# Reading the streamed operand from its last column down, with the split weights at shifting places, in a two-block transformer kernel

## The chip, the cores and the metric

The kernel runs on one core of one Trainium2 chip. The metric is the device time of one execution in microseconds. A comparison of two kernels on this problem tells differences of about 2% from no change.

## The reference

Two transformer blocks run one after the other on 256 tokens of width 2048, all in float32. The first has a gated linear recurrence, sliding-window attention and a feed-forward network with adaptive scales; the second a gated linear attention and a feed-forward network. Nearly all arithmetic is in products of 256 tokens with large weight matrices:

```python
h = modulate(rms_norm(x, norm1_g[l]), sh1, sc1)      # mod = silu(c) @ ada_w + ada_b
proj = h @ w_in[l] + b_in[l]
...
merged = gate_lru * (y_lru @ w_lru_out[l]) + gate_attn * (y_attn @ w_attn_out[l])
x = x + g1 * (merged @ w_o[l])
h2 = modulate(rms_norm(x, norm2_g[l]), sh2, sc2)
gate, up = jnp.split(h2 @ w_ffn_in[l], 2, axis=-1)
x = x + g2 * ((jax.nn.silu(gate) * up) @ w_ffn_out[l])
...
proj = h @ w_in                                       # second block, gla_w_in
...
return o.astype(h.dtype) @ w_out                      # gla_w_out
...
return (jax.nn.silu(g) * u) @ w_down                  # ffn_w_gu, ffn_w_down
```

## The kernel before

**Chunks.** Every large weight matrix is streamed once, in chunks of 512 input rows by 512 output columns (1 MB). `load` brings a chunk into `raw` (three buffers, on the SP queue). `split` turns it, in two halves of 128 x 1024, into two numbers of reduced precision that TensorE takes in one pass: ScalarE writes `hi`, a rounded copy (L165), and VectorE writes `lo = raw - hi` (L167). `hi` and `lo` have three buffers each. The activations lie in SBUF in the same form, `src.hi` and `src.lo`, four tiles of 256 tokens to a chunk.

**Matmuls.** `accumulate` adds a chunk's product to two PSUM banks, with three products in place of one: hi x hi, hi x lo, lo x hi. There are two forms:

- By token (`tokens=True`): the activations of 128 tokens are the stationary operand and 512 columns of weights stream past them. Lines 182, 183 and 184, 24 matmuls of 512 columns a chunk. The gate and up projections (`fgps`, `fups`), the values (`gvps`) and group 13 of `w_in` go this way.
- By feature: 128 columns of weights are stationary and the 256 tokens stream past. Lines 189, 191 and 193, 48 matmuls of 256 columns a chunk. All other weights go this way (`part`, `aops`, `ups`, `gps`, `glps`, `lops`, `wops`, `fops`, `gkps`, `gqps`, `grps`, `ggps`).

A group is the run of chunks whose products add up in the same two banks: 4 chunks mostly, 5 or 6 for `fops`. In all there are 464 chunks.

**Around the stream.** Small work (attention, the recurrence, norms) is cut into generators that `pump` advances between chunks. Their own matmuls, such as `sps` (L360, L361), `rps` (L570, L571) and `lrps` (L785 to L787, with 16 columns of weights), stand between those of the stream. The product of `c` with `ada_w` runs on VectorE: `matvec` loads a 512 KB strip into `mvw` (L234, pool of `MVS` buffers) and adds it, scaled, into `mva` (L239). Its first 16 steps come before any matmul; later ones are spread over the chunks, on the POOL queue and then on the SP queue between the loads of `raw`. A scheduler with priorities orders the instructions; `lead` moves the loads and splits ahead.

The pools around the change:

```python
SLOTS, MVS, RAWS, HIS, LOS = 24, 6, 3, 3, 3
mvw = ctx.enter_context(tc.tile_pool(name="mvw", bufs=MVS))
hip = ctx.enter_context(tc.tile_pool(name="hip", bufs=HIS))
lop = ctx.enter_context(tc.tile_pool(name="lop", bufs=LOS))
```

Of the kernel before, what the change touches and what calls it, by code (L numbers as in the profile page):

```python
# [12 lines left out]
F32R = mybir.dt.float32r  # L13
# [5 lines left out]
P = 128  # L19
# [3 lines left out]
NG = NK // 4  # L23
EPS = 1e-6
PREP = 2000
SLOTS, MVS, RAWS, HIS, LOS = 24, 6, 3, 3, 3
NEG = -3.0e38
HEADS = 16
KVH = 4
# [20 lines left out]
def block_pair_kernel(ctx: ExitStack, tc: tile.TileContext, a: dict):  # L50
    nc = tc.nc
# [7 lines left out]
    hip = ctx.enter_context(tc.tile_pool(name="hip", bufs=HIS))  # L59
    lop = ctx.enter_context(tc.tile_pool(name="lop", bufs=LOS))  # L60
# [8 lines left out]
    def f32(ap):  # L69
        return ap.bitcast(F32)  # L70
# [21 lines left out]
    def halves(t):  # L92
        return [t[:, 0:2, :], t[:, 2:4, :]]
# [56 lines left out]
    def load(ap):  # L150
        raw = rawp.tile([P, 4, 512], F32, tag="raw", name="raw")
        nc.sync.dma_start(raw, ap)
        return raw

    lead = [0]

    def split(ap):

        parts = []
        with tc.high_priority(offset=lead[0]):  # L160
            raw = load(ap)
            for b in range(2):
                rb = raw[:, 2 * b:2 * b + 2, :]
                hi = hip.tile([P, 2, 512], F32R, tag="hi", name="hi")
                nc.scalar.activation(hi, rb, AF.Copy)  # L165
                lo = lop.tile([P, 2, 512], F32R, tag="lo", name="lo")
                nc.vector.tensor_tensor(lo, rb, f32(hi), ALU.subtract)  # L167
                parts.append((hi, lo))
        return parts

    def accumulate(ps, ap, src, first, last, tokens=False):

        parts = split(ap)
        for kk in range(4):
            hi, lo = parts[kk // 2]
            wk = kk % 2
            fst, lst = first and kk == 0, last and kk == 3
            if tokens:
                for t in range(2):
                    tsl = slice(t * P, (t + 1) * P)  # L180
                    xh, xl = src.hi(kk)[:, tsl], src.lo(kk)[:, tsl]
                    nc.tensor.matmul(ps[t], xh, hi[:, wk, :], start=fst, stop=False)  # L182
                    nc.tensor.matmul(ps[t], xh, lo[:, wk, :], start=False, stop=False)  # L183
                    nc.tensor.matmul(ps[t], xl, hi[:, wk, :], start=False, stop=lst)  # L184
                continue
            for f in range(4):
                wsl = slice(f * P, (f + 1) * P)
                o = ps[f // 2][:, f % 2, :]
                nc.tensor.matmul(o, hi[:, wk, wsl], src.hi(kk), start=fst and f % 2 == 0,  # L189
                                 stop=False, skip_group_check=True)  # L190
                nc.tensor.matmul(o, hi[:, wk, wsl], src.lo(kk), start=False, stop=False,  # L191
                                 skip_group_check=True)
                nc.tensor.matmul(o, lo[:, wk, wsl], src.hi(kk), start=False, stop=lst,  # L193
                                 skip_group_check=True)

    def banks(name, tokens=False):
        return [bank(name, [P, 512] if tokens else [P, 2, T]) for _ in range(2)]

    def project(chunks, src, name, tokens=False):


        ps = banks(name, tokens)
        n = len(chunks)
        for c in range(n):
            accumulate(ps, chunks[c], src[c], c == 0, c == n - 1, tokens)
            if c < n - 1:
                pump()
        return ps

    def chunks_of(wname, g, ks=None):  # L210
        w = a[wname]
        return [w[g, k] for k in (range(w.shape[1]) if ks is None else ks)]
# [44 lines left out]
    def ada_steps(strip, queue=nc.gpsimd):  # L257


        def done(ps):  # L260
            if strip < 4:
                cols = ((16 + 4 * strip, 0, 4), (4 * strip, 4, 4))
            else:
                cols = ((8 * strip, 0, 8),)
            for j, p, n in cols:
                nc.vector.tensor_tensor(mod[:, j:j + n], ps[:, p:p + n], v("ada_b", j, n), ALU.add)

        return matvec([a["ada_w"][strip, k] for k in range(NK)], lambda k: cact[:, k:k + 1],
                      1024, done, queue)
# [149 lines left out]
    first = ada_steps(0, nc.sync)  # L419
# [36 lines left out]
    for q in range(NG):  # L456
# [3 lines left out]
        for g, ks in plan[q]:  # L460
            tok = g == 13
            if g in held:
                if q == 0:
                    early[g] = banks(f"e{g}", tok)
                ps = early[g]
            else:
                ps = banks("part")
            for k in ks:
                if g in held:
                    accumulate(ps, a["w_in"][g, k], h[k], k == 0, k == NG - 1, tok)  # L470
                else:
                    accumulate(ps, a["w_in"][g, k], h[k], k == ks[0], k == ks[-1])
                for st in ahead[:share]:
                    st()
                if ahead and len(ahead) <= share:
                    next_h()
                ahead = ahead[share:]
                lead[0] = PREP
                if q == NG - 1 and k < ks[-1]:
                    pump()  # L480
            if g not in held:
# [8 lines left out]
                ps = halves(early[g])  # L490
# [20 lines left out]
    for f in range(NG):  # L511
        ps = banks("aops")
# [96 lines left out]
    for f in range(NG):  # L609
# [4 lines left out]
        ps = project(chunks_of("w_lru_out", f), y_lru, "lops")  # L614
# [20 lines left out]
    for f in range(NG):  # L635
        ps = project(chunks_of("w_o", f), merged, "wops")
# [219 lines left out]
    for g in range(2):  # L856
        kg = slot("gk")
        ps = project(chunks_of("gla_w_in", 2 + g), h, "gkps")
# [6 lines left out]
        ps = project(chunks_of("gla_w_in", g), h, "gqps")  # L865
# [9 lines left out]
    for hd in range(GH):  # L875
        vg = slot("gv", shape=[P, 2, 512])
        ps = project(chunks_of("gla_w_in", 4 + hd), h, "gvps", True)
# [36 lines left out]
    for hd in range(GH):  # L914
        ps = project(chunks_of("gla_w_in", 8 + hd), h, "grps")
# [12 lines left out]
    for f in range(NG):  # L928
        ps = banks("ggps")
# [136 lines left out]
```

## Time and profile before

| | |
|---|---|
| time, median of 2 runs | 2779.15 us (2778.5 to 2779.8) |
| the profiled execution | 2775.35 us, span 2773.6 us |
| mean granted TensorE clock | 0.999 |
| busy: TensorE, weight loads, VectorE, ScalarE | 98%, 90%, 64%, 48% |
| moved by DMA | 602 MB, 217 GB/s in the mean |

The span runs from the first to the last instruction. A row of the timeline gives start and duration in microseconds, engine, line, operation, the tiles written and read, and shape and count. PE rows are matmuls, PEld rows the loads of the stationary operand. Matmuls are pipelined, so their durations overlap; how fast they go is read from start to start. A row of waits names who waited for whom, the sum in microseconds, the number of times and the longest.

### The profile page before, as it was taken

How to read it: one execution, taken by the hardware profiler on the slowest of the kernel's cores; microseconds unless marked ns; L12 is line 12 of the kernel's file. 1: busy time of each engine (PE TensorE's matmuls, PEld its weight loads, DVE VectorE, ACT ScalarE, POOL GpSimd, SP SyncE). 2: the span in 40 equal slices, each digit the busy share in tenths (PEclk: the TensorE clock that was granted, in tenths of full speed). 3: DMA queues.
4: the chain of work that ended last, by engine and by line, in shares of the span. 5: the costliest groups of instructions: out<-in, count | busy, mean ns of one | idle time of the engine just before them, and what ended most of it. 6: DMA issues, size and time to landing. Idle time of an engine off the chain costs nothing.

```text
span 2773.6 us, 43912 instructions
## 1 busy us (share of the span) xinstructions
PE 2710.8 (98%) x18612; PEld 2489.2 (90%) x18612; DVE 1784.8 (64%) x2000; ACT 1321.3 (48%) x1531; POOL 25.7 (1%) x52
## 2 busy tenths in 40 slices
PE   4999999999999999999999999999999999999999
PEld 4999899999999788899888999899988889988899
DVE  8887966977876865444444677866654444444544
ACT  3446537873445444434444555555554443344443
POOL 1100000000000000000000000000000000000000
PEclk9999999999999999999999999999999999999999
DMA  9974784768875776555555544445555555555554
GB/s 364 368 301 149 261 324 175 282 241 324 326 283 181 271 259 217 180 190 193 183 192 186 190 169 168 147 144 182 192 188 182 183 190 189 198 182 189 185 196 160
DMA packets 100165, 602.00 MB, mean 217 GB/s; under 512 B 11120, under 2 KB 11632, under 8 KB 40576
## 3 DMA queue, kind: packets, MB, share of 16 engines
q1 hardware_dynamic: 93056, 574.03, 58.2%
q0 software_dynamic: 6912, 25.17, 2.3%
q8 instruction: 145, 2.38, 0.3%
q14 instruction: 52, 0.43, 0.0%
HBM read 597.06 MB, written 2.10 MB: 216 GB/s over the span
## 4 chain that ended last, share of the span: by engine, by line
PE 91%; DVE 5%; ACT 1%; issue 1%; DMA 1%; SPq 0%; DVEq 0%; ACTq 0%
PE fops L189 6%; PE fops L191 6%; PE fops L193 6%; PE fgps L184 6%; PE fgps L183 6%; PE fgps L182 6%; PE fups L184 5%; PE fups L183 5%; PE fups L182 5%; DVE lo L167 2%; PE part L189 2%; PE part L191 2%; PE part L193 2%; DVE mva L239 1%; DMA mvw<-ada_w 1%
## 5 line engine op out<-in xcount | busy, mean ns | idle before, releaser
L167 DVE TENSOR_TENSOR lo<-raw,hi 128x1024 fp32r<-128x1024 f32 x928 | 1134.4, 1223 | 899.3 <-ACT hi L165 897.5
L165 ACT ACTIVATE hi<-raw 128x1024 fp32r<-128x1024 f32 x928 | 982.8, 1060 | 1285.8 <-PE fups L184 280.6
L189 PE MATMUL fops<-hid,hi 128*128 128x256 f32 x1408 | 389.0, 276 | 0.0
L193 PE MATMUL fops<-hid,lo 128*128 128x256 f32 x1408 | 388.8, 276 | 0.0
L191 PE MATMUL fops<-hid,hi 128*128 128x256 f32 x1408 | 388.8, 276 | 0.0
L183 PE MATMUL fups<-lo,h 128*128 128x512 f32 x704 | 275.9, 392 | 0.9 <-DVE lo L167 0.9
L184 PE MATMUL fups<-hi,h 128*128 128x512 f32 x704 | 276.7, 393 | 0.0
L182 PE MATMUL fups<-hi,h 128*128 128x512 f32 x704 | 274.2, 390 | 0.0
L184 PE MATMUL fgps<-hi,h 128*128 128x512 f32 x672 | 264.9, 394 | 0.0
L182 PE MATMUL fgps<-hi,h 128*128 128x512 f32 x672 | 264.6, 394 | 0.0
L191 PEld LDWEIGHTS fops<-hid,hi 128*128 128x128 f32 x1408 | 264.3, 188 | 0.0
L189 PEld LDWEIGHTS fops<-hid,hi 128*128 128x128 f32 x1408 | 264.3, 188 | 0.0
L193 PEld LDWEIGHTS fops<-hid,lo 128*128 128x128 f32 x1408 | 264.3, 188 | 0.0
L183 PE MATMUL fgps<-lo,h 128*128 128x512 f32 x672 | 263.3, 392 | 0.0
L239 DVE SCALAR_TENSOR_TENSOR mva<-mvw,cact,mva 128x1024 f32<-128x1024 f32 x180 | 230.2, 1279 | 18.7 <-DMA mvw<-ada_w 17.0
L183 PEld LDWEIGHTS fups<-lo,h 128*128 128x128 f32 x704 | 132.2, 188 | 31.3 <-DVE lo L167 1.3
L182 PEld LDWEIGHTS fups<-hi,h 128*128 128x128 f32 x704 | 132.2, 188 | 29.3
L184 PEld LDWEIGHTS fups<-hi,h 128*128 128x128 f32 x704 | 132.3, 188 | 27.4
L183 PEld LDWEIGHTS fgps<-lo,h 128*128 128x128 f32 x672 | 126.3, 188 | 27.4
L182 PEld LDWEIGHTS fgps<-hi,h 128*128 128x128 f32 x672 | 126.3, 188 | 26.3
L184 PEld LDWEIGHTS fgps<-hi,h 128*128 128x128 f32 x672 | 126.3, 188 | 26.0
L189 PE MATMUL part<-h,hi 128*128 128x256 f32 x512 | 145.6, 284 | 0.1
(322 smaller groups left out, 5440.6 us busy)
## 6 DMA issues: line engine op xcount, KB each, us to landing
raw<-w_in SPq DMA_DIRECT2D x88, 1024.0 KB, 4.9
raw<-w_ffn_in SPq DMA_DIRECT2D x88, 1024.0 KB, 4.8
raw<-ffn_w_gu SPq DMA_DIRECT2D x88, 1024.0 KB, 4.8
mvw<-ada_w SPq DMA_DIRECT2D x144, 512.0 KB, 6.5
raw<-gla_w_in SPq DMA_DIRECT2D x48, 1024.0 KB, 4.8
raw<-w_ffn_out SPq DMA_DIRECT2D x44, 1024.0 KB, 4.9
raw<-ffn_w_down SPq DMA_DIRECT2D x44, 1024.0 KB, 4.9
mvw<-ada_w POOLq DMA_DIRECT2D x48, 512.0 KB, 8.4
```

The costliest lines, as they stand in the source:

```text
L165: nc.scalar.activation(hi, rb, AF.Copy)
L167: nc.vector.tensor_tensor(lo, rb, f32(hi), ALU.subtract)
L182: nc.tensor.matmul(ps[t], xh, hi[:, wk, :], start=fst, stop=False)
L183: nc.tensor.matmul(ps[t], xh, lo[:, wk, :], start=False, stop=False)
L184: nc.tensor.matmul(ps[t], xl, hi[:, wk, :], start=False, stop=lst)
L189: nc.tensor.matmul(o, hi[:, wk, wsl], src.hi(kk), start=fst and f % 2 == 0, stop=False, skip_group_check=True)
L191: nc.tensor.matmul(o, hi[:, wk, wsl], src.lo(kk), start=False, stop=False, skip_group_check=True)
L193: nc.tensor.matmul(o, lo[:, wk, wsl], src.hi(kk), start=False, stop=lst, skip_group_check=True)
L239: nc.vector.scalar_tensor_tensor(state["acc"], w, col(k), state["acc"], ALU.mult, ALU.add)
```

## The change

The matmuls of `accumulate` take the moving operand with a step of -1, from the last column to the first, and address the PSUM bank in the same manner, so that each result lands where it did. The stationary operand is taken as before. The buffers of `hi` and `lo` get 128 elements more, and `halfbuf` puts the half at one of four starts in its buffer, 0, 16, 32 or 48 elements; `next_place` chooses a pair of starts for each group, sixteen pairs in turn, counted apart for the two forms. The room for it comes from `mvw`, which has five buffers in place of six.

```diff
-SLOTS, MVS, RAWS, HIS, LOS = 24, 6, 3, 3, 3
+SLOTS, MVS, RAWS, HIS, LOS = 24, 5, 3, 3, 3
...
+    place = {}
+    groups = [0, 0]
+
+    def next_place(tokens):
+        n = groups[tokens]
+        groups[tokens] += 1
+        place["hi"], place["lo"] = 16 * (n % 4), 16 * ((n // 4 + n) % 4)
+
+    def halfbuf(pool, name):
+        t = pool.tile([P, 1024 + P], F32R, tag=name, name=name)
+        return t[:, place[name]:place[name] + 1024].rearrange("p (b n) -> p b n", b=2)
+
     def split(ap):
...
-                hi = hip.tile([P, 2, 512], F32R, tag="hi", name="hi")
+                hi = halfbuf(hip, "hi")
                 nc.scalar.activation(hi, rb, AF.Copy)
-                lo = lop.tile([P, 2, 512], F32R, tag="lo", name="lo")
+                lo = halfbuf(lop, "lo")
                 nc.vector.tensor_tensor(lo, rb, f32(hi), ALU.subtract)
...
     def accumulate(ps, ap, src, first, last, tokens=False):
 
+        if first:
+            next_place(tokens)
         parts = split(ap)
...
-                    nc.tensor.matmul(ps[t], xh, hi[:, wk, :], start=fst, stop=False)
-                    nc.tensor.matmul(ps[t], xh, lo[:, wk, :], start=False, stop=False)
-                    nc.tensor.matmul(ps[t], xl, hi[:, wk, :], start=False, stop=lst)
+                    o, wh, wl = ps[t][:, ::-1], hi[:, wk, ::-1], lo[:, wk, ::-1]
+                    nc.tensor.matmul(o, xh, wh, start=fst, stop=False)
+                    nc.tensor.matmul(o, xh, wl, start=False, stop=False)
+                    nc.tensor.matmul(o, xl, wh, start=False, stop=lst)
                 continue
+            xh, xl = src.hi(kk)[:, ::-1], src.lo(kk)[:, ::-1]
             for f in range(4):
                 wsl = slice(f * P, (f + 1) * P)
-                o = ps[f // 2][:, f % 2, :]
-                nc.tensor.matmul(o, hi[:, wk, wsl], src.hi(kk), start=fst and f % 2 == 0,
+                o = ps[f // 2][:, f % 2, ::-1]
+                nc.tensor.matmul(o, hi[:, wk, wsl], xh, start=fst and f % 2 == 0,
                                  stop=False, skip_group_check=True)
-                nc.tensor.matmul(o, hi[:, wk, wsl], src.lo(kk), start=False, stop=False,
+                nc.tensor.matmul(o, hi[:, wk, wsl], xl, start=False, stop=False,
                                  skip_group_check=True)
-                nc.tensor.matmul(o, lo[:, wk, wsl], src.hi(kk), start=False, stop=lst,
+                nc.tensor.matmul(o, lo[:, wk, wsl], xh, start=False, stop=lst,
                                  skip_group_check=True)
```

The added lines move everything below them by 17 lines: L189, L191 and L193 become L206, L208 and L210, and L234 becomes L251.

The scheduler's order changes at a few places. The first is the SP queue at the start, with the waits that each load has. The DVE wait is for VectorE to free the buffer. Before:

```order
L97 DMA vec<-vec 128x436
L234 DMA mvw<-ada_w 128x1024 x6
L234 DMA mvw<-ada_w 128x1024 [waits DMAHW1_49,DVE_49]
L234 DMA mvw<-ada_w 128x1024 [waits DMAHW2_49,DMAHW0_49,DVE_49]
L234 DMA mvw<-ada_w 128x1024 [waits DMAHW3_49,DVE_49]
L234 DMA mvw<-ada_w 128x1024 [waits DMAHW4_49,DVE_49]
L423 DMA x_84<-xT 128x1024
```

After the change:

```order
L97 DMA vec<-vec 128x436
L251 DMA mvw<-ada_w 128x1024 x5
L251 DMA mvw<-ada_w 128x1024 [waits DMAHW1_49,DVE_49]
L251 DMA mvw<-ada_w 128x1024 [waits DMAHW2_49,DVE_49]
L251 DMA mvw<-ada_w 128x1024 [waits DMAHW3_49,DMAHW0_49,DVE_49]
L251 DMA mvw<-ada_w 128x1024 [waits DMAHW4_49,DVE_49]
L251 DMA mvw<-ada_w 128x1024 [waits DMAHW5_49,DVE_49]
L440 DMA x_84<-xT 128x1024
```

Five loads go out at once where it was six; the sixth waits for VectorE.

The second place is on TensorE, in the recurrence of the first block: `gps` is the stream, `rps` the two gate products of the recurrence (for each of four heads a pair). Before:

```order
L193 MATMUL gps<-h,lo 128x256
L189 MATMUL gps<-h,hi 128x256
L570 MATMUL rps<-uc,lw 128x256
L571 MATMUL rps<-uc,lw 128x256
L191 MATMUL gps<-h,hi 128x256
L193 MATMUL gps<-h,lo 128x256
L189 MATMUL gps<-h,hi 128x256
```

After the change:

```order
L206 MATMUL gps<-h,hi 128x256
L208 MATMUL gps<-h,hi 128x256
L587 MATMUL rps<-uc,lw 128x256
L588 MATMUL rps<-uc,lw 128x256
L587 MATMUL rps<-uc,lw 128x256
L588 MATMUL rps<-uc,lw 128x256
L210 MATMUL gps<-h,lo 128x256
```

The four pairs of this group stood at four places among the matmuls of the stream and now stand two by two. Elsewhere TensorE has the same sequence as before; on VectorE some steps of `mva` and `lo` change places with their neighbours.

## The prediction, made before the changed kernel was run

> **What bounds the kernel now.** I read the page from the top: busy times, slices, chain, then the groups.
>
> ```profile
> PE 2710.8 (98%) x18612; PEld 2489.2 (90%) x18612; DVE 1784.8 (64%) x2000; ACT 1321.3 (48%) x1531; POOL 25.7 (1%) x52
> ...
> PEclk9999999999999999999999999999999999999999
> ...
> PE 91%; DVE 5%; ACT 1%; issue 1%; DMA 1%; SPq 0%; DVEq 0%; ACTq 0%
> ...
> PE mvp L251 <- DVE mva L239: 36.7, 3, 34.4
> ...
> raw<-w_in SPq DMA_DIRECT2D x88, 1024.0 KB, 4.9
> ```
>
> TensorE is busy 98% of the 2773.6 us span, with 91% of the chain that ended last, and its granted clock is at the top in every slice. It stands idle at the start (34.4 us until the first matmul) and in small pieces later. So what counts is the rate at which TensorE takes matmuls. A busy matmul is pipelined: its duration overlaps the next, and the rate is the distance from start to start. That I read from the timeline, first and last row of an answer, in four stretches without waits:
>
> ```profile
> 1199.82 0.28 PE L189 MATMUL fops<-hid,hi 128*128 128x256 f32 x1
> ...
> 1221.92 0.28 PE L189 MATMUL fops<-hid,hi 128*128 128x256 f32 x1
> ```
>
> These are 196 feature matmuls (256 columns): 22.10 us over 195 distances, 113.3 ns each.
>
> ```profile
> 631.78 0.28 PE L193 MATMUL lops<-yr,lo 128*128 128x256 f32 x1
> ...
> 653.92 0.28 PE L191 MATMUL glps<-h,hi 128*128 128x256 f32 x1
> ```
>
> The same shape, 189 rows: 22.14 us over 188, 117.8 ns. So there are two paces, and a stretch keeps its pace for many chunks.
>
> ```profile
> 1469.81 0.39 PE L183 MATMUL fgps<-lo,h 128*128 128x512 f32 x1
> ...
> 1505.97 0.39 PE L182 MATMUL fups<-hi,h 128*128 128x512 f32 x1
> ...
> 154.43 0.40 PE L182 MATMUL e<-hi,h 128*128 128x512 f32 x1
> ...
> 159.33 0.40 PE L182 MATMUL e<-hi,h 128*128 128x512 f32 x1
> ```
>
> Token matmuls (512 columns): 36.16 us over 158 distances is 228.9 ns; in the early stretch 4.90 us over 21 is 233.3 ns. Going from 256 to 512 columns doubles the distance (113.3 to 228.9), so the price is per column, 0.443 to 0.447 ns, with no fixed part to save.
>
> The code gives the counts: 464 chunks of weights, of which 196 are taken by token (22 gate and 22 up groups of 4, 4 v groups of 4, and the 4 chunks of group 13), 24 matmuls each, 4,704; the other 268 by feature, 48 each, 12,864. At their faster paces they take 12,864 x 113.3 = 1457.9 us and 4,704 x 228.9 = 1076.7 us, together 2534.6 of the span. How much of the slower pace is mixed in shows in the mean durations, which follow the pace (276 where the distance is 113.3, 281 where it is 117.8):
>
> ```profile
> L191 PE MATMUL fops<-hid,hi 128*128 128x256 f32 x1408 | 388.8, 276 | 0.0
> L191 PE MATMUL lops<-yr,hi 128*128 128x256 f32 x256 | 71.9, 281 | 0.0
> L191 PE MATMUL wops<-m,hi 128*128 128x256 f32 x256 | 71.9, 281 | 0.0
> L191 PE MATMUL glps<-h,hi 128*128 128x256 f32 x256 | 71.9, 281 | 0.0
> L191 PE MATMUL ups<-h,hi 128*128 128x256 f32 x256 | 71.2, 278 | 0.0
> L191 PE MATMUL part<-h,hi 128*128 128x256 f32 x512 | 143.0, 279 | 0.0
> ```
>
> lops, wops and glps are slow throughout: three lines of 256 each, 2,304 matmuls x 4.4 ns = 10 us. ups, gps and part lie about halfway, some 3,000 matmuls at 1.5 to 2.5 ns, 5 us more. So the slow pace costs about 15 us today.
>
> **The change part by part.**
>
> *Direction.* All 17,568 weight matmuls read the moving operand and address the bank from the last column down. No matmul is added, and each result lands where it did. The trace has no operand that runs down, so the price is unknown and I bound it. Three rows stand near:
>
> ```profile
> 213.53 0.60 PE L361 MATMUL sps<-kT,e 128*128 128x256 f32 x2
> 213.97 0.38 PE L360 MATMUL sps<-kT,e 128*128 128x128 f32 x2
> ...
> L785 PEld LDWEIGHTS lrps<-h,warh x16: 93/94/98, 1643.1 to 1649.1; 128*16 128x16 f32 x16
> L785 PE MATMUL lrps<-h,warh x16: 276/276/362, 1643.1 to 1649.2; 128*16 128x256 f32 x16
> ```
>
> The two sps records of 256 columns, plain f32, take 0.44 us from start to start, 0.22 each: the slowest streaming of 256 columns here, and my upper end (each column fetched or written by itself). [...] Nearest of all is the unchanged pace: same bytes, same number of columns, still one run without gaps. I take 0.
>
> [...]
>
> *Places.* The halves start 0, 16, 32 or 48 elements later in their buffers, another pair for each of sixteen groups in turn. In feature matmuls they are the stationary operand, in token matmuls the moving one. If the weight load disturbed the stream, a short load should show a better pace. The lrps rows are that case: 16 columns of weights, loads of 94 ns in place of the 188 of fops, and yet 276 ns, the duration that goes with 113.3. So the load next to the stream doesn't set the pace, and I take 0 for feature groups. In token groups every place lies a whole number of 64 bytes from the old one; I take 0, and as bounds the two token paces, 4.4 ns a matmul or 21 us in all, which are counted under the next point.
>
> *Which pace a stretch gets.* Fast and slow stretches use the same tiles; the pace changes where other matmuls stand between:
>
> ```profile
> 521.23 0.28 PE L189 MATMUL gps<-h,hi 128*128 128x256 f32 x1
> ...
> 527.23 0.28 PE L189 MATMUL gps<-h,hi 128*128 128x256 f32 x1
> 528.12 0.67 PE L570 MATMUL rps<-uc,lw 128*128 128x256 f32 x2 [0.61 <-ACT hi L165]
> ...
> 540.04 0.28 PE L189 MATMUL gps<-h,hi 128*128 128x256 f32 x1
> ...
> 546.05 0.28 PE L193 MATMUL gps<-h,lo 128*128 128x256 f32 x1
> ```
>
> Before the rps pair 51 distances take 6.00 us (117.6 ns); a dozen microseconds behind it 53 take 6.01 (113.4). At this very place the order now puts the four rps pairs two by two, where before they stood at four places. I read the pace as a state into which TensorE falls at an interruption, so the change draws it anew: between the 15 us saved if all is fast, and, if all is slow, 12,864 x 117.8 - 1473 = +42 us and 4,704 x 233.3 - 1077 = +21 us. I take 0.
>
> *Splitting.* hi and lo are the same 928 instructions each on ScalarE and VectorE, with rows of the same length: 0.
>
> *Five buffers instead of six for ada_w.*
>
> ```profile
> SPq L152 <- DVE lo L167: 2328.9, 453, 17.2
> SPq L234 <- DVE mva L239: 47.2, 28, 4.7
> ...
> POOL mvw L234 <- DVE mva L239: 95.9, 45, 27.2
> ...
> L239 DVE SCALAR_TENSOR_TENSOR mva<-mvw,cact,mva 128x1024 f32<-128x1024 f32 x180 | 230.2, 1279 | 18.7 <-DMA mvw<-ada_w 17.0
> ```
>
> An mvw load now waits for the step five back on VectorE, not six, so it issues up to one step (1.28 us) later. Behind it on the SP queue stand the loads of raw, for which ScalarE and then TensorE wait. The cover is that SP waits 2328.9 us for lo to free raw buffers: it runs well ahead. At the lower end the cost is 0; at the upper, all 144 loads of the SP queue late by a step with no cover, 184 us. VectorE waits only 17 us for these loads today, which lies by the lower end: +2 us, most of it before the first matmul.
>
> **Sum.** Against the profiled execution, 2775.4 us (span 2773.6 and 1.8 around it): 0 + 0 + 0 + 0 + 2 = 2777. The two timed runs have a median of 2779.15, 3.8 above, so I forecast 2780, and 2755 to 2830 for this case. A measurement of this kernel tells about 2% (2723.6 and 2834.7) from no change.
>
> **Rivals.**
>
> *The slow pace everywhere.* Descending, or shifted by 64 bytes, the stream can't fall into the fast state. Place: every weight matmul. Price +63 us, 2842; it turns the verdict to slower once some nine tenths of the matmuls are affected. For it: two paces exist and the tiles don't explain them. Against: the fast one holds for most of the run, over all tiles.
>
> [...]
>
> [...]
>
> **How the numbers follow.** No effect beyond the draw of the pace: 0.59. Slow everywhere: 0.11. One column at a time or a milder loss: 0.16. Less friction: 0.14. Faster 0.14, same 0.59, slower 0.27. The range takes in the forecast's own, the slow pace and the frictionless case, 0.84, and leaves out one column at a time: 2670 to 2850. The 184 us of the buffers stay outside, as covered.
>
> **What would show it.** Right: distances of 113 or 118 and of 229 or 233 ns again, the same in all sixteen combinations, and groups with means of 276 to 284 and 390 to 394. Wrong: any other distance, or a distance that goes with the place. Wrong on the buffers: TensorE idle behind mvw, above 5 us in sum. A 512-column matmul at 0.44 us would mean one column at a time.

## The result, and the profile after

The changed kernel takes 2846.17 us (median of 2 runs, 2844.74 to 2847.6) against 2779.15: a ratio of 1.0237 (95% interval 1.022 to 1.0254), **slower**. That is inside the range that was given, but not where the forecast stood: 2780 us and no change. It is 4 us above the rival "the slow pace everywhere" (2842), which had a chance of 0.11, and 4 us under the top of the range, 2850.

The page of the changed kernel, the lines that answer to those of before (busy times, clock slices, engines on the chain that ended last):

```profile
PE 2785.9 (98%) x18612; PEld 2545.2 (89%) x18612; DVE 1790.3 (63%) x2000; ACT 1322.2 (46%) x1531; POOL 25.8 (1%) x52
...
PEclk9999999999999999999999999999999999999999
...
PE 92%; DVE 4%; DMA 2%; issue 1%; ACT 1%; POOL 0%; SPq 0%; DVEq 0%; POOLq 0%; ACTq 0%
...
L210 PE MATMUL fops<-hid,lo 128*128 128x256 f32 x1408 | 398.5, 283 | 0.0
L208 PE MATMUL fops<-hid,hi 128*128 128x256 f32 x1408 | 396.0, 281 | 0.0
...
L199 PE MATMUL fups<-lo,h 128*128 128x512 f32 x704 | 279.4, 397 | 0.0
```

The instruction counts are those of before, TensorE is as full as before, and the granted clock stays in the top tenth. What changed is the duration of a matmul: 281 to 283 ns where `fops` had 276, and 397 for this line of `fups`, which had 392 and for which the prediction set 390 to 394.

The pace itself, from start to start, comes from the timeline of the changed kernel: first and last row of four stretches without waits. Two feature stretches, with `hi` and `lo` both 0 elements into their buffers, and both 16; then two token stretches, `hi` at 32 with `lo` at 16, and both at 16.

```profile
1211.75 0.28 PE L206 MATMUL fops<-hid,hi 128*128 128x256 f32 x1
...
1232.95 0.28 PE L206 MATMUL fops<-hid,hi 128*128 128x256 f32 x1
1245.79 0.28 PE L208 MATMUL fops<-hid,hi 128*128 128x256 f32 x1
...
1266.91 0.28 PE L206 MATMUL fops<-hid,hi 128*128 128x256 f32 x1
1337.76 0.40 PE L199 MATMUL fups<-lo,h 128*128 128x512 f32 x1
...
1357.82 0.40 PE L198 MATMUL fups<-hi,h 128*128 128x512 f32 x1
1407.83 0.40 PE L200 MATMUL fgps<-hi,h 128*128 128x512 f32 x1
...
1427.94 0.40 PE L198 MATMUL fgps<-hi,h 128*128 128x512 f32 x1
```

They are 180 distances in 21.20 us, 176 in 21.12, 86 in 20.06 and 85 in 20.11: 117.8, 120.0, 233.3 and 236.6 ns. Over the whole run no pair of places has a mean below 117.8 for features or below 233.3 for tokens. The 113.3 and 228.9 ns of before have gone.

Adding up all distances of the trace (a distance far above the pace counts as a wait, less one pace) says where the 72.2 us between the spans come from. The other kernels of this table are those of the experiments below.

| | feature matmuls, mean ns (x12,863) | token matmuls, mean ns (x4,704) | waits, us | span, us |
|---|---|---|---|---|
| before | 114.53 | 229.04 | 43.3 | 2773.6 |
| after | 118.74 | 233.50 | 40.5 | 2845.8 |
| places alone, upward | 117.3 | 231.08 | about 40 | 2817.2 |
| direction alone | 118.22 | 233.28 | 35.0 | 2832.9 |
| upward, one pair of places a form | 113.5 | 227.02 | 45.1 | 2755.0 |

Features give +54.1 us (4.21 ns x 12,863), tokens +21.0 (4.46 ns x 4,704), waits -2.8: 72.3 of the 72.2.

The waits of the changed kernel (who waited for whom, sum in us, times, longest) show the five `mvw` buffers:

```profile
SPq L251 <- DVE mva L256: 59.7, 34, 4.7
...
POOL mvw L251 <- DVE mva L256: 65.9, 39, 4.1
...
PE mvp L268 <- DVE mva L256: 36.3, 2, 34.0
```

The SP queue waits 59.7 us for a buffer where it was 47.2, the POOL queue 65.9 where it was 95.9, and the first matmul still comes 34.0 us in. VectorE and ScalarE are as busy as before (1790.3 and 1322.2 us against 1784.8 and 1321.3).

### The profile page after: what moved, and what is told of

Same layout as the page of the kernel before. It is cut to its first block, busy times and chain, and to the rows that moved or that the text cites. A ratio compares the mean times of both kernels' runs of the same rounds, so it can differ in the third digit from the quotient of the medians.

```text
span 2845.8 us, 43930 instructions
## 1 busy us (share of the span) xinstructions
PE 2785.9 (98%) x18612; PEld 2545.2 (89%) x18612; DVE 1790.3 (63%) x2000; ACT 1322.2 (46%) x1531; POOL 25.8 (1%) x52
## 4 chain that ended last, share of the span: by engine, by line
PE 92%; DVE 4%; DMA 2%; issue 1%; ACT 1%; POOL 0%; SPq 0%; DVEq 0%; POOLq 0%; ACTq 0%
PE fops L210 6%; PE fops L206 6%; PE fops L208 6%; PE fgps L198 6%; PE fgps L200 6%; PE fgps L199 6%; PE fups L200 5%; PE fups L198 5%; PE fups L199 5%; PE part L208 2%; PE part L206 2%; DVE lo L180 2%; PE part L210 2%; DMA mvw<-ada_w 2%; PE grps L208 1%
## 5 line engine op out<-in xcount | busy, mean ns | idle before, releaser
L210 PE MATMUL fops<-hid,lo 128*128 128x256 f32 x1408 | 398.5, 283 | 0.0
L206 PE MATMUL fops<-hid,hi 128*128 128x256 f32 x1408 | 397.2, 282 | 0.0
L208 PE MATMUL fops<-hid,hi 128*128 128x256 f32 x1408 | 396.0, 281 | 0.0
L198 PE MATMUL fups<-hi,h 128*128 128x512 f32 x704 | 279.3, 397 | 0.0
L200 PE MATMUL fups<-hi,h 128*128 128x512 f32 x704 | 279.3, 397 | 0.0
L198 PE MATMUL fgps<-hi,h 128*128 128x512 f32 x672 | 269.7, 401 | 0.0
L200 PE MATMUL fgps<-hi,h 128*128 128x512 f32 x672 | 267.7, 398 | 0.0
L208 PEld LDWEIGHTS fops<-hid,hi 128*128 128x128 f32 x1408 | 265.6, 189 | 0.0
L206 PEld LDWEIGHTS fops<-hid,hi 128*128 128x128 f32 x1408 | 265.0, 188 | 0.0
L210 PEld LDWEIGHTS fops<-hid,lo 128*128 128x128 f32 x1408 | 264.5, 188 | 0.0
L206 PE MATMUL part<-h,hi 128*128 128x256 f32 x512 | 148.1, 289 | 0.0
```

Of the source, the lines that this page charges most:

```text
L198: nc.tensor.matmul(o, xh, wh, start=fst, stop=False)
L200: nc.tensor.matmul(o, xl, wh, start=False, stop=lst)
L206: nc.tensor.matmul(o, hi[:, wk, wsl], xh, start=fst and f % 2 == 0, stop=False, skip_group_check=True)
L208: nc.tensor.matmul(o, hi[:, wk, wsl], xl, start=False, stop=False, skip_group_check=True)
L210: nc.tensor.matmul(o, lo[:, wk, wsl], xh, start=False, stop=lst, skip_group_check=True)
```

## Experiments

The questions were: direction or places? If direction, the read of the moving operand or the write of the bank? And what about a place matters? The first four kernels answer the first two questions; they ran on one chip beside 13 runs of the kernel before, median 2777.3 us. Most differences here are under the 2% at which two kernels are told apart on this problem, so each ratio is read with its interval.

### Places alone, upward

The changed kernel with the three reversals taken out:

```diff
-                    o, wh, wl = ps[t][:, ::-1], hi[:, wk, ::-1], lo[:, wk, ::-1]
+                    o, wh, wl = ps[t], hi[:, wk, :], lo[:, wk, :]
...
-            xh, xl = src.hi(kk)[:, ::-1], src.lo(kk)[:, ::-1]
+            xh, xl = src.hi(kk), src.lo(kk)
...
-                o = ps[f // 2][:, f % 2, ::-1]
+                o = ps[f // 2][:, f % 2, :]
```

> The direction undone, the sixteen places and the five mvw buffers kept. Theory D (the direction alone sets the pace): back to 113.3 or 117.8 ns a feature matmul and 228.9 to 233.3 a token matmul, the same for every place; 2770 to 2785 us. Theory P (the places of the weights meet the other stream, whatever its direction): the pace differs by place as in the changed kernel, 117.8 to 120 ns and 233.3 to 235; 2830 to 2850 us. Between them, about 2810 us, if each has half of the 72 us.

2820.5 us, ratio 1.0156 (1.0141 to 1.0171): without the direction the places, with the five `mvw` buffers, cost 43 us. The pace now goes with the place. Four stretches of its timeline: features at (0, 0), features at (32, 32), tokens at (32, 32), tokens at (48, 48), the place of `hi` first.

```profile
1200.80 0.28 PE L206 MATMUL fops<-hid,hi 128*128 128x256 f32 x1
...
1221.99 0.28 PE L208 MATMUL fops<-hid,hi 128*128 128x256 f32 x1
1267.74 0.28 PE L208 MATMUL fops<-hid,hi 128*128 128x256 f32 x1
...
1288.94 0.28 PE L208 MATMUL fops<-hid,hi 128*128 128x256 f32 x1
1414.72 0.39 PE L199 MATMUL fups<-lo,h 128*128 128x512 f32 x1
...
1435.95 0.39 PE L200 MATMUL fups<-hi,h 128*128 128x512 f32 x1
1439.82 0.39 PE L199 MATMUL fgps<-lo,h 128*128 128x512 f32 x1
...
1459.79 0.39 PE L200 MATMUL fgps<-hi,h 128*128 128x512 f32 x1
```

187 distances of 113.3 ns, 180 of 117.8, 91 of 233.3 and 88 of 226.9. The last is faster than anything in the kernel before. Features at (0, 32) have 113.6 in the mean, at (16, 16) 118.7, at (48, 48) 119.9.

The place doesn't explain everything. One group of `gps`, at (0, 0) throughout, begins at one pace and goes on at the other after matmuls of `rps`, the last of them from 540.72 to 542.26:

```profile
527.21 0.28 PE L206 MATMUL gps<-h,hi 128*128 128x256 f32 x1
...
532.65 0.28 PE L206 MATMUL gps<-h,hi 128*128 128x256 f32 x1
542.57 0.28 PE L210 MATMUL gps<-h,lo 128*128 128x256 f32 x1
...
552.82 0.28 PE L210 MATMUL gps<-h,lo 128*128 128x256 f32 x1
```

These are 48 distances of 113.3 ns and 87 of 117.8.

### Direction alone

The kernel before, with moving operand and bank reversed as in the change, the halves where they were and six `mvw` buffers.

```diff
-                    nc.tensor.matmul(ps[t], xh, hi[:, wk, :], start=fst, stop=False)
+                    o, wh, wl = ps[t][:, ::-1], hi[:, wk, ::-1], lo[:, wk, ::-1]
+                    nc.tensor.matmul(o, xh, wh, start=fst, stop=False)
...
+            xh, xl = src.hi(kk)[:, ::-1], src.lo(kk)[:, ::-1]
...
-                o = ps[f // 2][:, f % 2, :]
+                o = ps[f // 2][:, f % 2, ::-1]
```

> Direction changed, places and the six mvw buffers as before. Theory D: all feature matmuls at 117.8 ns, all token matmuls at 233.3, as the changed kernel has them where both halves start at 0: 12,864 x 117.8 and 4,704 x 233.3 give 2836 to 2840 us. Theory P: the paces of before, 2775 to 2785 us.

2832.02 us, ratio 1.0196 (1.0179 to 1.0213): the direction costs 54.7 us by itself. A feature and a token stretch of its timeline:

```profile
1167.76 0.28 PE L192 MATMUL fops<-hid,hi 128*128 128x256 f32 x1
...
1188.96 0.28 PE L192 MATMUL fops<-hid,hi 128*128 128x256 f32 x1
1442.69 0.40 PE L185 MATMUL fgps<-lo,h 128*128 128x512 f32 x1
...
1483.99 0.40 PE L185 MATMUL fups<-lo,h 128*128 128x512 f32 x1
```

180 distances in 21.20 us are 117.8 ns, 177 in 41.30 are 233.3. So the slow paces come with the direction, without any shift. Here too one place has two of them: some feature groups, the last eight of `fops` among them, go at 120.0 ns, which brings the mean to 118.22. The two parts don't add: 54.7 + 43.2 would be 97.9, and the whole change costs 67.0 by the medians of the first comparison.

### The bank alone, and the read alone

In the first kernel only the bank is addressed downward, in the second only the moving operand is read downward; in each the columns of a product land in reversed order.

```diff
# the bank alone
-                o = ps[f // 2][:, f % 2, :]
+                o = ps[f // 2][:, f % 2, ::-1]
...
# the read alone
+            xh, xl = src.hi(kk)[:, ::-1], src.lo(kk)[:, ::-1]
```

The token form is edited in the same way in both.

> Only the bank is addressed from the last column down; the moving operand runs up, so that tokens, or columns, land in reversed order (the sums are other than the reference's). If the write into PSUM makes the pace: 117.8 and 233.3 ns, about 2838 us. If the read of the moving operand makes it: 113.3 and 228.9 ns, about 2779 us. If it is both together that matter, something between.

> Only the moving operand is read from the last column down; the bank runs up, so that tokens, or columns, land in reversed order. If the read makes the pace: 117.8 and 233.3 ns, about 2838 us. If the write makes it: 113.3 and 228.9 ns, about 2779 us.

The bank alone: 2777.12 us, ratio 1.0 (0.999 to 1.001). The read alone: 2831.61 us, 1.0196 (1.0175 to 1.0216). The groups of instructions, of the bank alone first:

```profile
L192 PE MATMUL fops<-hid,hi 128*128 128x256 f32 x1408 | 389.0, 276 | 0.0
...
L184 PE MATMUL fups<-hi,h 128*128 128x512 f32 x704 | 274.3, 390 | 0.0
```

The same groups of the read alone:

```profile
L192 PE MATMUL fops<-hid,hi 128*128 128x256 f32 x1408 | 397.4, 282 | 0.0
...
L184 PE MATMUL fups<-hi,h 128*128 128x512 f32 x704 | 279.1, 396 | 0.0
```

All of the direction's price lies in the read (1.0196, as with both reversed); a descending bank costs nothing (1.0).

### A shorter stationary operand

Does the stream slow down because it reads beside the load of the stationary operand? In these two kernels all chunks of a group but the first and the last load 16 columns in place of 128, once downward and once upward, and the sums of the other rows are left out.

```diff
+            w = P if fst or lst else 16
...
-                    tsl = slice(t * P, (t + 1) * P)
+                    tsl = slice(t * P, t * P + w)
...
-                wsl = slice(f * P, (f + 1) * P)
+                wsl = slice(f * P, f * P + w)
```

> As the kernel with the direction alone, but the stationary operand has 16 columns in place of 128, except in the first and the last tile of a group: most of the sums are left out, the streams are as long as before. Theory W (the weight load beside the stream takes turns with it at the memory): the short load meets it an eighth as often, and the pace falls to 113.3 ns or below for 256 columns, to 226 or below for 512. Theory S (the stream alone makes the pace, whatever loads beside it): 118 and 233 ns stay.

> As the kernel before, with the stationary operand cut to 16 columns in the same manner. Theory W: no slow stretches at 117.8 ns any more, 113.3 or below throughout, and token matmuls at 226.7 or below. Theory S: two paces, 113.3 and 117.8, and 228.9 as before.

Downward 2830.12 us and upward 2783.37, one run each, where 128 columns gave 2832.02 (on the chip of the first four kernels) and 2778.91. The groups by form, downward first, with the load of the stationary operand in the last row:

```profile
L193 PE MATMUL fops<-hid,hi 128*16 128x256 f32 x1280 | 358.4, 280 | 0.0
...
L185 PE MATMUL fups<-hi,h 128*16 128x512 f32 x616 | 244.2, 396 | 0.0
...
L193 PEld LDWEIGHTS fops<-hid,hi 128*16 128x16 f32 x1280 | 120.3, 94 | 29.7
```

Upward:

```profile
L190 PE MATMUL fops<-hid,hi 128*16 128x256 f32 x1280 | 353.3, 276 | 0.0
...
L183 PE MATMUL fups<-hi,h 128*16 128x512 f32 x616 | 243.5, 395 | 0.0
```

The load takes 94 ns where the full one takes 188. From one 16-column matmul to the next the means are 117.79 and 233.33 ns downward, where direction alone had 118.22 and 233.28: the short load doesn't bring the fast paces back. Upward they are 114.1 and 231.6 ns, where the kernel before had 114.5 and 229.0. So neither expectation came for tokens upward: the shorter load makes them slower, by 2.5 ns, in all their groups alike (the 395 above was 390). The length of the load isn't the cause of the slow downward read, but it is not without effect.

### Everything moved by 64 bytes

The kernel before with 16 elements of padding ahead of the activations and the weights, so that both start 64 bytes later:

```diff
+    pad = ctx.enter_context(tc.tile_pool(name="pad", bufs=1))
+    nc.vector.memset(pad.tile([P, 16], F32, name="pad"), 0.0)
```

> The kernel before, with 64 bytes (16 elements) put ahead of the pool of activations, so that activations and weights both lie 64 bytes further on. If the pace goes by where the two operands lie to each other: 113.3 or 117.8 and 228.9 ns, 2775 to 2785 us. If it goes by the place of the weights alone: as the places (16, 16) had it upward, 118.7 and 232.4 ns, 2845 to 2850 us.

2777.2 us, ratio 0.9992 (0.9982 to 1.0002), means of 114.5 and 229.05 ns, and the groups of before:

```profile
L191 PE MATMUL fops<-hid,hi 128*128 128x256 f32 x1408 | 389.0, 276 | 0.0
...
L184 PE MATMUL fups<-hi,h 128*128 128x512 f32 x704 | 274.3, 390 | 0.0
```

Moving one operand by 64 bytes costs (features at (16, 16) in the first experiment: 118.7 ns, against a mean of 114.53 before); moving both costs nothing (114.5 and 229.05 ns). At least for this shift, what counts is how the two operands lie to each other, not where they lie. That both did move follows from the order of the pools; the trace shows no addresses.

### One pair of places for each form, upward

From the first experiment I took the pairs with the best means: (0, 32) for features, (48, 48) for tokens, the other code as in that kernel, five `mvw` buffers included.

```diff
-        place["hi"], place["lo"] = 16 * (n % 4), 16 * ((n // 4 + n) % 4)
+        place["hi"], place["lo"] = (48, 48) if tokens else (0, 32)
```

> Upward, with one fixed pair of places for each form, the best of the sixteen: feature groups hi at 0 and lo at 32, token groups both at 48. If the paces of the sixteen places hold when a place is used alone: 12,864 x 113.6 and 4,704 x 227.0 ns, 12 and 9.6 us under the kernel before, 2755 to 2760 us. If the neighbours' places made them, 2770 to 2785 us.

2757.7 us (6 runs, 2755.54 to 2763.69), ratio 0.9928 (0.9914 to 0.9942): this is **faster than both kernels**. The gain is under 2%, but the interval leaves out 1, and the slowest of the six runs lies under the fastest of the 17 of the kernel before on this chip (2775.36). A feature and a token stretch of its timeline:

```profile
1142.79 0.28 PE L203 MATMUL fops<-hid,hi 128*128 128x256 f32 x1
...
1163.98 0.28 PE L205 MATMUL fops<-hid,hi 128*128 128x256 f32 x1
1453.67 0.40 PE L197 MATMUL fgps<-hi,h 128*128 128x512 f32 x1
...
1493.81 0.39 PE L197 MATMUL fups<-hi,h 128*128 128x512 f32 x1
```

187 distances of 113.3 ns and 177 of 226.8. Over the run the means are 113.5 and 227.02: features save 13.3 us, because almost no stretch is slow any more, and tokens 9.5, because of a pace that the kernel before never had.

### How far the places repeat, and how fine they are

Three kernels, run once each, map the place. The first puts both halves at nine places 64 bytes apart, upward; the second moves by single elements around the good places, upward; the third by single elements from 0, downward.

```diff
# 64 bytes apart, upward
+        place["hi"] = place["lo"] = 16 * (n % 9)
# single elements, upward
+        j = n % 16
+        place["hi"], place["lo"] = (48 + j, 48 + j) if tokens else (j, 32 + j)
# single elements, downward
+        place["hi"] = place["lo"] = n % 16
```

> Upward, both halves at the same place, 0, 16, 32 and so on to 128 elements, another for each group. If the pace goes by the distance of the two operands modulo 256 bytes: 64 and 128 repeat 0 (113.3 or 117.8 ns; 229.0), 80 repeats 16 (118.7; 232.4), 96 repeats 32 (117.8; 233.3), 112 repeats 48 (119.9; 227.0). If modulo 512 bytes: 64 to 112 have paces of their own, 128 repeats 0. If by the whole address: none repeats.

> Upward, the best pairs of places moved on by 0 to 15 elements, another for each group: feature groups (0 + j, 32 + j), token groups (48 + j, 48 + j). If whole blocks of 64 bytes decide: every j like 0, 113.5 and 226.9 ns, or j over 0 dearer by one block, up to 1.7 ns more. If single lines of 16 bytes decide: steps at j = 4, 8 and 12, with paces between 113 and 120, 227 and 236. [...]

> Downward, both halves at the same place, 0 to 15 elements, another for each group. If running down only moves the meeting of the two operands to other places: some j gets back to 113.3 and 227 ns, as upward. If running down has a price of its own: no j comes under 117.8 and 233.3 ns, and the others lie above, up to about 120 and 240; 2840 to 2860 us.

They took 2822.23, 2835.93 and 2859.55 us, beside one run of the kernel before for each: 2779.21 for the first two, 2783.07 for the third. Steps of 64 bytes, token means in ns:

| place | 0 | 16 | 32 | 48 | 64 | 80 | 96 | 112 | 128 |
|---|---|---|---|---|---|---|---|---|---|
| mean | 229.5 | 232.3 | 233.3 | 227.0 | 229.0 | 232.6 | 233.3 | 227.1 | 229.1 |

Two stretches of that kernel's timeline, at places 112 and 128:

```profile
1373.75 0.40 PE L198 MATMUL fups<-hi,h 128*128 128x512 f32 x1
...
1393.95 0.39 PE L200 MATMUL fups<-hi,h 128*128 128x512 f32 x1
1397.63 0.39 PE L198 MATMUL fgps<-hi,h 128*128 128x512 f32 x1
...
1416.86 0.39 PE L198 MATMUL fgps<-hi,h 128*128 128x512 f32 x1
```

89 distances of 227.0 ns and 84 of 228.9: the pace of 48 comes back at 112, that of 0 at 64 and 128. (At 0 two of the 21 chunks go at 233.3 and 233.5 ns and lift the mean; the others lie near 229.) Features do the same: 118.8 ns at 16 and 80, 119.9 at 48 and 112. In steps of 64 bytes the pattern so repeats every 64 elements, 256 bytes. Features at 0, 32, 64 and 128 have groups at 113.3 and at 117.8 ns and neither confirm nor contradict it.

Within these, single elements count. Two token stretches of the second kernel, at places 48 and 49:

```profile
1381.81 0.40 PE L199 MATMUL fups<-hi,h 128*128 128x512 f32 x1
...
1401.99 0.39 PE L201 MATMUL fups<-hi,h 128*128 128x512 f32 x1
1405.70 0.40 PE L199 MATMUL fgps<-hi,h 128*128 128x512 f32 x1
...
1425.92 0.40 PE L200 MATMUL fgps<-lo,h 128*128 128x512 f32 x1
```

89 distances of 226.7 ns, and 85 of 237.9 one element (4 bytes) further. The means of places 48 to 63 lie between 227.0 and 239.5 for tokens, of (0, 32) to (15, 47) between 113.6 and 120.0 for features. No stretch goes below 113.3 and 226.7. Neither expectation, whole blocks or lines, fits: the steps come from one element to the next, not only at 4, 8 and 12, and tokens reach 239.5, above the 236 that lines were given.

Downward, the means lie between 117.8 and 120.0 for features and 233.3 and 242.1 for tokens. Two token stretches, at places 15 and 0:

```profile
1367.77 0.41 PE L200 MATMUL fgps<-hi,h 128*128 128x512 f32 x1
...
1386.91 0.40 PE L198 MATMUL fgps<-hi,h 128*128 128x512 f32 x1
1389.80 0.40 PE L198 MATMUL fups<-hi,h 128*128 128x512 f32 x1
...
1410.80 0.40 PE L198 MATMUL fups<-hi,h 128*128 128x512 f32 x1
```

79 distances of 242.3 ns and 90 of 233.3. Places can make the downward read worse; no place tried makes it better than 117.8 and 233.3, 4.0% above 113.3 and 2.9% above 226.7. So the second expectation came. Tried with both halves alike were 19 of the 64 places in 256 bytes (0 to 15 here; 16, 32 and 48 in the changed kernel); that the downward read has a floor of its own is likely, not shown.

## Why the prediction was right and wrong

**The number: inside the range by luck.** The forecast was 2780 us and no change, with 2755 to 2830 for that case, which 2846.17 misses by 16 us. The range reaches to 2850 only because it takes in the rival "the slow pace everywhere", and the result lies 4 us inside that edge. The two terms that were put at 0 for the change itself, direction and places, both failed.

**What bounds the kernel: right.** TensorE's rate decided all; features and tokens hold 75.1 us of the slowdown, waits took 2.8 back.

**Direction, "I take 0": wrong, and the largest error.** Alone it costs 54.7 us (ratio 1.0196). The value was drawn from sameness: as many bytes and columns, one run without gaps. No row of before had a descending operand, and the upper end, 0.22 us for 256 columns (the `sps` records), lay about 105 ns above the mean of before, while the effect was 3.7 of 114.5 ns for a feature matmul and 4.2 of 229.0 for a token matmul, by the means of direction alone. The step that failed is the one from sameness to 0; what a few nanoseconds each are worth the prediction knew (+63 us for the slow pace everywhere). The runs show the price in the read of the moving operand: ratio 1.0196 (1.0175 to 1.0216) for the read alone.

**The descending bank, part of that 0: right.** No row of before had one, so the prediction had no measurement to go by. The bank alone gives 2777.12 us, a ratio of 1.0 (0.999 to 1.001). The price lay on the other side, in the read.

**Places, "0": wrong.** The step was: a short load beside the stream shows 276 ns, so the load next to the stream doesn't set the pace, so its place doesn't either. The second half doesn't follow from the first, and the first holds only in part: downward a load of 94 ns leaves the paces nearly as they were (117.79 and 233.33 ns against 118.22 and 233.28), upward it moves tokens from 229.0 to 231.6 ns. The `lrps` rows also hold more than their duration of 276 ns shows. In the timeline of before they run at 117.2 ns (18 distances from 1643.34 to 1645.45) and, after an interruption (a wait and `tokps`, 0.75 us), at 113.3 (24 from 1646.72 to 1649.44). Their stationary operand moves on by 64 bytes after every third matmul, and in the second stretch none of the four places costs anything. So with 16 columns the place made no difference in this form, while with 128 it did (113.6 ns at (0, 32), 119.9 at (48, 48), upward); how length and place act together no run shows. Upward the places cost 43 us; on top of the direction, by the spans, 12.9 us (2845.8 against 2832.9), of which about 6.7 are feature matmuls (0.52 ns x 12,863), 1.0 token matmuls and 5.5 waits. That "every place lies a whole number of 64 bytes from the old one" was no protection: the pattern is 256 bytes long (token means of 229.5, 232.3, 233.3, 227.0 and 229.0 ns at 0, 16, 32, 48 and 64 elements). How the two operands lie to each other moves a token matmul from 226.7 to 237.9 ns, and a load half as long moves it from 229.0 to 231.6.

**"A state into which TensorE falls": partly right.** One group at (0, 0) upward passes from 113.3 to 117.8 ns across the `rps` matmuls, and `lrps` from 117.2 to 113.3 across `tokps`, so the pace does change at interruptions. But it isn't a free draw. The changed kernel never reached the fast pace (no mean below 117.8 and 233.3 ns), and with features at (0, 32) the run is almost all fast (113.5). What the prediction listed as a sign of error, "a distance that goes with the place", is what the profile showed.

**The rival "the slow pace everywhere": nearly what came.** Of its two conditions the descending read held everywhere. The shift by itself did not: upward, features at (0, 32) and tokens at (48, 48) are fast (113.5 and 227.02 ns). Its price was +63 us; measured were 75.1 for the matmuls, because many features go at up to 120.0 rather than 117.8. Its argument against, that the fast pace holds over all tiles, held only for the upward read and the tiles' old places. The range's lower end, 2670 us, and the chance of 0.14 on "less friction" count on paces under 113.3 and 226.7 ns; no run shows one, those two being the fastest stretches at any place tried. The 0.16 on "one column at a time or a milder loss" counts on much slower matmuls, up to 0.44 us for 512 columns; no run shows these either, the slowest stretches being 120.0 ns for 256 columns and 242.3 for 512.

**Splitting and buffers: right as far as shown.** 0 for the splits (busy times above). No run takes the five buffers alone. Waits fell by 2.8 us in all, but a slower TensorE waits less: they are 35.0 us with direction alone and six buffers, against 43.3 before. At equal direction the kernels with five buffers wait longer, 45.1 against 43.3 us upward and 40.5 against 35.0 downward, with the places changed as well. That is of the size of the +2 us, and TensorE's wait for `mva` is as before (36.3 us against 36.7, nearly all of it ahead of the first matmul).

**Open.** Why the downward read is slower, whether one of the 45 places not tried would spare it, and how the two addresses act on each other, no run shows. Nor does any show what in an interruption makes one pair of places pass from one pace to the other, nor why a shorter load slows tokens upward. Reading the stationary operand downward as well was not tried.

## What to carry to other kernels

In a kernel that is a stream of thousands of matmuls on a full TensorE, measure the distance from start to start to a tenth of a nanosecond before calling a new addressing free: 4 ns each was 2% here, and mean durations (276 against 282) already showed it. Read the moving operand upward (downward the whole kernel took 1.0196 times as long); if it must be mirrored, mirror the write of the bank, which cost nothing (1.0). Where the two operands lie to each other is worth a sweep over 256 bytes: the right pair of places gave 0.7%, the sixteen pairs in turn cost 1.6%.

## What the runs showed of the hardware that I had not expected

- Reading the moving operand downward costs 2 to 3% of a matmul at unchanged places (means of 118.2 against 114.5 ns for 256 columns, 233.3 against 229.0 for 512), and 3 to 4% against the fastest place found (117.8 against 113.3, 233.3 against 226.7). Writing the bank downward costs nothing (1.0, 0.999 to 1.001).
- The pace of a matmul depends on how its two operands lie to each other, with a period of 256 bytes in steps of 64 (token means of 229.0 and 229.1 ns at 64 and 128 elements, 227.0 and 227.1 at 48 and 112), and with differences from one element to the next (226.7 and 237.9 ns for neighbouring places), though a common shift of 64 bytes doesn't matter (0.9992, 0.9982 to 1.0002).
- A shorter load of the stationary operand (94 in place of 188 ns) doesn't bring the fast paces back downward (117.79 and 233.33 ns) and slows token matmuls upward (231.6 against 229.0).
- At one pair of places the pace can pass from 113.3 to 117.8 ns where other matmuls interrupt the stream, and then holds for chunks (87 distances here).
- Upward, the fastest paces found, 113.3 and 226.7 ns, are both 0.443 ns a column; the kernel before already ran its features there for most of the time (mean 114.53), and its tokens in no stretch (mean 229.04).
